# A two-layer encoder on one core: state products from split operands, and a key-norm sum in another PSUM bank

## The chip, the cores and the metric

One NeuronCore of one Trainium2 chip runs the whole program. Its engines have a queue each and meet through semaphores: TensorE (PE in the profile, its weight loads PEld), VectorE (DVE), ScalarE (ACT), GpSimd (POOL), and SyncE (SP), which issues nearly all DMAs. The metric is the device time of one execution in microseconds; less is better.

## The reference, cut to what matters

Two sequences of 512 tokens, each behind 16 learned tokens (528 columns), go through two layers of width 1024.

Layer 1 is a bidirectional gated delta rule with 8 heads. Per head and direction a state `S` (128 x 256) is carried over chunks of tokens, and each chunk uses it twice, with its keys and with its queries:

```
v_new = u_c - w_c @ S
o = qg_c @ S + attn_c @ v_new
S = S * exp(gl_c) + kd_c.T @ v_new
```

Layer 2 is attention with 16 heads; its keys are normalised per head before the scores:

```
k = concatenate([k_nope, k_pe]);  k = k * rsqrt(mean(k * k) + eps) * gain
o = softmax(q @ k.T * scale) @ v
```

The result has to be accurate, so most products are made of split operands: a float32 value is written as a high part `H` (rounded to float32r) and a low part `L` (the rest), and a product is the sum of three float32r passes, H*H, L*H and H*L. A product of plain float32 operands is one instruction in the program and two in the profile.

## The kernel before, in words

Instructions are recorded in Python order and then ordered for every engine by a planner with a timing model of its own; an earlier recorded instruction has priority, those under `high_priority` (helper `pri`) are taken as if recorded so many places earlier, and the planner may take any later recorded one whose inputs and buffers are ready. On the chip each engine then runs its list strictly in that order. `issue_after(x)` makes what is recorded under it stand behind `x` on x's engine. Buffers belong to tags (`BUFS1`, `BUFS2` in SBUF, `PBUFS1`, `PBUFS2` for PSUM banks); a tag with one buffer serves its users in turn.

**Layer 1** (`run`, loop over i from 0 to 15) has 16 units, 8 heads for each of the two sequences. For unit i the scan `gdn_scan` is recorded under high priority, and between its ten steps (5 chunks, 2 directions) pieces of later units are recorded as filling: `gdn_front(i+2)`, which projects, convolves and prepares keys and queries (tile `kq`, conv at L364), `gdn_v(i+1)`, `gdn_z(i+1)`, and under i = 14 and 15 the output projection `out_proj` of the first sequence. A scan starts by splitting two tiles per direction (`kd`, `at`: high part on ACT at L663, low part on POOL through helper `sub`, L87). Each step then goes from engine to engine:

- L682, PE: keys times `S`, plain float32, into bank `ch0` or `ch1`; L684, DVE: `r`
- L693, PE: `r` times the chunk's inverse; L696, ACT, and L697, DVE: its high and low part `vH`, `vL`
- L700, PE: queries times `S`, plain float32, into bank `po`
- L80 to L82, PE (helper `mm3v`): three passes with `vH`, `vL` for the new state and three for the output; L709, DVE: the new `S` (in the first chunk L707, a copy on ACT)
- L719 and L720: the output is taken from `po` and summed.

Projections are streams of float32r passes (helper `mm3`, L74 to L76) into the two banks of tag `pj`; their weights are loaded by SP, rounded by ACT (L213), and their low part is made by POOL (L87).

**Layer 2** (`head`, `pair_scores`, `pair_out`) works by pairs of heads, 16 pairs over both sequences. While the eight tiles of scores of one pair are worked on, the next pair is prepared in steps. `pair_k` projects the keys, ACT and POOL make their squares (L961 to L963), PE sums these over the channels (L966) into the one bank of tag `x`, DVE scales the sums (L967), POOL takes the root (L91), and two DMAs write the result `rk` to DRAM and read it back over all partitions as `rs`. `pair_knorm` multiplies with `rs`: the rope part `kp` on POOL (L1033), then its split `kst` on ACT (L1035); the keys on DVE (L1030), then their split `kH` on ACT. It is recorded in `head` behind two instructions: the last weight split on POOL (`last_wl`) and the last maximum of scores on DVE (`last_mx`). `pair_z` evicts its projection from a `pj` bank by ACT and DVE (L1046, L1047). Bank `x` also serves `pair_out` (the product with the values, L74 to L76 and L1099, released by DVE at L1100) and `pair_q` (L995).

Of the kernel before, what the change touches and what calls it, by code (L numbers as in the profile page):

```python
# [17 lines left out]
T = 528  # L18
# [5 lines left out]
class Trunk:  # L24
    def __init__(self, ctx, tc, ins, outs):
        self.tc, self.nc, self.ins, self.outs = tc, tc.nc, ins, outs
        self.ctx = ctx
        self.cn = ctx.enter_context(tc.tile_pool(name="cn", bufs=1))
        self.dr = ctx.enter_context(tc.tile_pool(name="dr", space=DRAM, bufs=1))
        self.sa = ctx.enter_context(tc.tile_pool(name="sa", bufs=1, reuse_waits="tile"))  # L30
        self.n = 0
        self.inner = None
        self.last_mx = None
        self.next_pool(self.BUFS1, self.PBUFS1)

    def next_pool(self, bufs, pbufs):
        if self.inner is not None:
# [4 lines left out]
        self.ps = self.inner.enter_context(self.tc.tile_pool(name="ps", space=PSUM, bufs=1, reuse_waits="tile"))  # L42

    BUFSA = dict(hnH=1, hnL=1, wraw=3, wh=3, wl=3, acc=4, raw=2)
    BUFS1 = dict(kq=4, kd0=2, kd1=2, kn=3, qe=4, bp=4, ssq=2, vt=2, zs=3, T1=1, X1=1, ms=3,
                 D=2, B=2, Dm=2, Q=1, oa=2, S0=1, S1=1, r=2, ot=1, vH=3, vL=3, osq=2, y=2, ss=4, rs=4, sq=2, 
                 beta=2, gg=2, gh=2, gl=2, ex=2, ne=2, gm=2)
    BUFS2 = dict(sqr=2, kss=2, ce=2, rk=2, sqH=1, sqL=1, kH=3, kL=3, qH=3, qL=3, kst=2, zs=3, qs=4, P=2, SQ0=2, SQ1=2, mx=3, sm=3)
    PBUFS2 = dict(pj=2, S=2, tr=1, x=1)
    PBUFS1 = dict(pj=2, tr=2, lv=1, ch0=1, ch1=1, po=1)  # L50
# [578 lines left out]
    def gdn_scan(self, u, yd, pend):  # L629
        nc = self.nc  # L630
        V, A, PE = nc.vector, nc.scalar, nc.tensor
        h, g, kq, kd, ms, qe, bp, at, XF, vt, zs = (
            u[k] for k in ("h", "g", "kq", "kd", "ms", "qe", "bp", "at", "XF", "vt", "zs"))
        ex = g["ex"]
        yv = yd[2 * h:2 * h + 2].rearrange("k p c -> p k c")
        at_tile = {i: (c0, n) for i, c0, n in self.tiles()}

        def out(i):
            c0, n = at_tile[i]
            sq = self.mO if i == 4 else self.t("osq", [128, 256])  # L640
            m = 80 if i == 4 else 128
            ss = self.t("ss", [128, 1])
            A.activation(sq[:n], oa[:n, i], AF.Square, accum_out=ss[:n])
            V.tensor_scalar(ss[:n], ss[:n], 1.0 / 256, qe[:n, i:i + 1], op0=ALU.mult, op1=ALU.add)
            rs = self.t("rs", [128, 1])
            self.rsqrt(rs[:n], ss[:n])
            A.activation(sq[:n], oa[:n, i], AF.Copy, scale=rs[:n])
            ps = self.p("po", [128, 2, m])
            for hf in range(2):
                PE.transpose(ps[:, hf], sq[:m, 128 * hf:128 * hf + 128], self.ident[:m, :m])  # L650
            y = self.t("y", [128, 2, 128])
            V.tensor_tensor(y[:, :, 0:n], ps[:, :, 0:n], zs[:, :, c0:c0 + n], op=ALU.mult)
            nc.sync.dma_start(yv[:, :, c0:c0 + n], y[:, :, 0:n])

        oa = self.t("oa", [128, 5, 256])
        G = nc.gpsimd
        at2, kd2 = [], []
        for d in range(2):
            n = 3 + d
            for nm, src, m, res in (("kd", kd[d], n, kd2), ("at", at[:, 4 * d:4 * d + 4], 4, at2)):  # L660
                hi = self.t("%sH%d" % (nm, d), [128, m, 128], F32R)
                lo = self.t("%sL%d" % (nm, d), [128, m, 128], F32R)
                A.copy(hi[:, 0:m], src[:, 0:m])  # L663
                self.sub(G, lo[:, 0:m], src[:, 0:m], hi[:, 0:m])
                res.append((hi, lo))
        mW, mR, mV = self.mW, self.mR, self.mV
        A.copy(mW[0:16], ms)
        A.copy(mW[32:48], ms)
        self.sub(V, mW[64:80], ms, mW[0:16])
        seen = set()  # L670
        S = [self.t("S%d" % d, [128, 256]) for d in range(2)]
        order = ([4, 0, 1, 2, 3], [3, 2, 1, 0, 4])
        for k in range(5):
            for d in range(2):
                i = order[d][k]
                n = NM if i == 4 else 128
                c0 = 0 if i == 4 else NM + 128 * i
                sl = slice(c0, c0 + n)
                pc = self.p("ch%d" % d, [128, 2, 256])
                r = vt[:n, i]  # L680
                if k > 0:
                    PE.matmul(pc[:n, 0], kq[:, 0, sl], S[d], start=True, stop=True)  # L682
                    r = self.t("r", [128, 256])[:n]
                    V.scalar_tensor_tensor(r, pc[:n, 0], g["ne"][:n, d, i, h:h + 1], vt[:n, i], op0=ALU.mult, op1=ALU.add)  # L684
                b = bp[:n, i, d:d + 1]
                if i == 4:
                    self.stack(mR, r)
                    PE.matmul(pc[:n, 1], mW[:, 32 + 16 * d:48 + 16 * d], mR, start=True, stop=True)
                    A.activation(mV[0:16], pc[:n, 1], AF.Copy, scale=b)
                    A.activation(mV[64:80], pc[:n, 1], AF.Copy, scale=b)  # L690
                    V.scalar_tensor_tensor(mV[32:48], pc[:n, 1], b, mV[0:16].bitcast(F32), op0=ALU.mult, op1=ALU.subtract)
                else:
                    PE.matmul(pc[:n, 1], XF[:, 4 * d + i], r, start=True, stop=True)  # L693
                    vH = self.t("vH", [128, 256], F32R)
                    vL = self.t("vL", [128, 256], F32R)
                    A.activation(vH, pc[:, 1], AF.Copy, scale=b)  # L696
                    V.scalar_tensor_tensor(vL, pc[:, 1], b, vH.bitcast(F32), op0=ALU.mult, op1=ALU.subtract)  # L697
                po = self.p("po", [128, 2, 256])
                if k > 0:
                    PE.matmul(po[:n, 0], kq[:, 1, sl], S[d], start=True, stop=True)  # L700
                if k < 4:
                    if i == 4:
                        PE.matmul(pc[:, 0], mW[:, 64:192], mV, start=True, stop=True)
                    else:
                        self.mm3v(pc[:, 0], [x[:, i] for x in kd2[d]], (vH, vL))
                    if k == 0:
                        A.copy(S[d], pc[:, 0])  # L707
                    else:
                        V.scalar_tensor_tensor(S[d], S[d], ex[:, 2, d, i, h:h + 1], pc[:, 0], op0=ALU.mult, op1=ALU.add)  # L709
                if i == 4:  # L710
                    PE.matmul(po[:n, 1], mW[:, 16 * d:16 * d + 16], mV, start=True, stop=True)
                else:
                    self.mm3v(po[:, 1], [x[:, i] for x in at2[d]], (vH, vL))
                e = ex[:n, 0, d, i, h:h + 1]
                if k == 0:
                    A.copy(oa[:n, i], po[:n, 1])
                else:
                    t = self.t("ot", [128, 256])[:n] if i in seen else oa[:n, i]
                    A.copy(t, po[:n, 1])  # L719
                    V.scalar_tensor_tensor(t, po[:n, 0], e, t, op0=ALU.mult, op1=ALU.add)  # L720
                    if i in seen:
                        G.tensor_tensor(oa[:n, i], oa[:n, i], t, op=ALU.add)  # L722
                seen.add(i)
                yield
            ready = pend if k == 0 else {3: [1], 4: [0, 2]}.get(k, [])
            for f in ready:
                f() if k == 0 else out(f)
        pend[:] = [lambda i=i: out(i) for i in (3, 4)]
# [217 lines left out]
    def pair_k(self, u):  # L946
# [8 lines left out]
        for j, h in enumerate(hs):  # L955
# [5 lines left out]
            A.activation(kk[o], kr[nn, j], AF.Square)  # L961
            A.activation(sq[o], kr[o, j], AF.Square)
            G.tensor_tensor(kk[o], kk[o], sq[o], op=ALU.add)  # L963
        ps = self.p("x", [88, 6, 2])
        for i in range(6):
            PE.matmul(ps[:, i], kk[:, 88 * i:88 * i + 88], self.two, start=True, stop=True)  # L966
        V.scalar_tensor_tensor(rk, ps.rearrange("p i j -> p j i"), 1.0 / 192, c["kss"].unsqueeze(1).to_broadcast([88, 2, 6]), op0=ALU.mult, op1=ALU.add)  # L967
# [81 lines left out]
    def pair_scores(self, u, j, qt):  # L1049
# [15 lines left out]
        V.tensor_scalar(mx, mx, qs[j][:, qt:qt + 1], None, op0=ALU.mult)  # L1065
        P = self.t("P", [128, 2, 264])
        sm = self.t("sm", [128, 1])
        A.activation(P, Sv, AF.Exp, bias=mx, scale=qs[j][:, qt:qt + 1], accum_out=sm)  # L1068
        V.reciprocal(sm, sm)
        P = P.rearrange("p a b -> p (a b)")  # L1070
        V.tensor_scalar(P, P, sm, None, op0=ALU.mult)
# [32 lines left out]
    def run(self, rc, rs):  # L1104
# [27 lines left out]
        v, z, inv = (lambda i: self.gdn_v(U[i])), (lambda i: self.gdn_z(U[i])), (lambda i: self.gdn_inverse(U[i]))  # L1132
        for f in (front(0), front(1), self.pri(inv(0), 1000), v(0), z(0)):
            drain(f)
        tL1 = ("kq", "kq", "kq", "B", "B", "zs", "vt", "oa")
        tA, tC = ("hnH", "hnL"), ("h2H", "h2L")
        rsd = [self.d("rsd", [1, T]) for _ in range(2)]
        pss = [[], []]
# [9 lines left out]
        for i in range(16):  # L1148
# [11 lines left out]
            for n, _ in enumerate(self.pri(self.gdn_scan(U[i], y1[units[i][0]], pend), 100)):  # L1160
                if n > 0:
                    next(iv, None)
                for _ in range(((1, 1, 1, 1, 1, 1, 1, 1, 1, 1) if i == 15 else (3, 3, 1, 2, 1, 2, 2, 3, 2, 2))[n]):
                    next(fill, None)
            drain(iv)
            if i != 15:
# [14 lines left out]
        def head(u):  # L1181
# [10 lines left out]
                yield  # L1192
            self.pair_q(u, 1)
            with ExitStack() as behind:
                for x in [self.last_wl] + ([self.last_mx] if self.last_mx is not None else []):
                    behind.enter_context(self.tc.issue_after(x.ins))
                self.pair_knorm(u, 0)
                self.pair_knorm(u, 1)
# [105 lines left out]
```

## Time and profile before

| | before |
|---|---|
| median of 3 runs | 2698.04 us (2696.45 to 2699.07) |
| profiled execution, time | 2700.19 us |
| profiled execution, span of its trace | 2698.5 us |
| TensorE clock granted, mean share | 0.957 |
| busy: PE, PEld, DVE, ACT, POOL | 93%, 83%, 65%, 54%, 47% |

Busy PE time counts matmuls that overlap in the array, so 93% is not 93% of its rate. Layer 1 fills the span to about 1350 us, layer 2 the rest. The rate of a stream is read from the starts of its instructions in the timeline, not from their durations. Times in queries are counted from the start of the span.

### The profile page before, as it was taken

Reading aid. Unit: us, or ns where it says so; the run is one execution under the profiler, and the core shown is the slowest. Engines: PE = TensorE matmul, PEld = TensorE weight load, DVE = VectorE, ACT = ScalarE, POOL = GpSimd, SP = SyncE. Lnnn points to the kernel's source line nnn. Section 1 sums busy time; section 2 is a strip of 40 time slices with the busy share of each in tenths; the row PEclk is TensorE's granted clock in tenths of the full one; section 3 lists DMA queues with packets and bytes.
Section 4 is the critical chain, followed back from the end, with each engine's and each line's share of the span. In section 5 each row is a group of like instructions: output and inputs, shape, how many; then the busy total and the mean of one; then the engine's idle time right before and its main releaser. Section 6 shows DMA issues by size and latency. Waiting matters only on the chain. (4 is left out here: it accounts for less than half of the span.)

```text
span 2698.5 us, 51896 instructions
## 1 busy us (share of the span) xinstructions
PE 2500.3 (93%) x19083; PEld 2237.2 (83%) x19083; DVE 1755.9 (65%) x3915; ACT 1452.6 (54%) x3522; POOL 1270.0 (47%) x1255
## 2 busy tenths in 40 slices
PE   8899999999999999899999999998998989999999
PEld 7888888878888888788989888887887878887787
DVE  6888887777897777886554356555665656566421
ACT  5445555556555555645545466555556555655432
POOL 5544554435445444533445555444436454544243
PEclk9999999989999999989999899999999999999999
DMA  3222222221222243225475423232322322225475
GB/s 101 67 51 59 56 62 57 70 61 48 62 63 59 53 125 83 78 70 152 121 229 160 125 73 80 67 66 73 91 79 76 79 67 71 66 66 152 136 231 148
DMA packets 448511, 245.14 MB, mean 91 GB/s; under 512 B 131132, under 2 KB 408878, under 8 KB 448256
## 3 DMA queue, kind: packets, MB, share of 16 engines
q1 hardware_dynamic: 448256, 241.82, 33.6%
q8 instruction: 150, 2.46, 0.4%
q14 instruction: 105, 0.86, 0.1%
HBM read 190.72 MB, written 42.08 MB: 86 GB/s over the span
## 5 line engine op out<-in xcount | busy, mean ns | idle before, releaser
L87 POOL TENSOR_TENSOR wl<-wraw,wh 128x512 fp32r<-128x512 f32 (+2 forms) x512 | 661.5, 1294 | 805.4 <-ACT wh L213 744.4
L74 PE MATMUL pj<-hnH,wh 128*128 128x264 f32 (+4 forms) x2080 | 634.1, 306 | 20.0 <-DVE zs L624 10.6
L76 PE MATMUL pj<-hnH,wl 128*128 128x264 f32 (+3 forms) x2080 | 633.6, 306 | 0.5 <-POOL wl L87 0.5
L75 PE MATMUL pj<-hnL,wh 128*128 128x264 f32 (+3 forms) x2080 | 628.9, 303 | 4.5 <-DVE hnL L774 4.5
L213 ACT CAST wh<-wraw 128x512 fp32r<-128x512 f32 (+2 forms) x512 | 306.9, 602 | 312.7 <-PE pj L75 203.2
L74 PEld LDWEIGHTS pj<-hnH,wh 128*128 128x128 f32 (+1 forms) x2080 | 402.5, 194 | 37.6 <-DVE zs L624 12.5
L75 PEld LDWEIGHTS pj<-hnL,wh 128*128 128x128 f32 (+1 forms) x2080 | 402.7, 194 | 18.6 <-DVE hnL L774 5.1
L76 PEld LDWEIGHTS pj<-hnH,wl 128*128 128x128 f32 (+1 forms) x2080 | 401.9, 193 | 15.5 <-issue 3.7
L74 PE MATMUL pj<-h2H,wh 128*128 128x512 f32 (+1 forms) x544 | 207.0, 383 | 5.0 <-ACT h2H L769 3.0
L76 PE MATMUL pj<-h2H,wl 128*128 128x512 f32 (+1 forms) x544 | 207.3, 382 | 0.0
L75 PE MATMUL pj<-h2L,wh 128*128 128x512 f32 (+1 forms) x544 | 206.2, 380 | 0.7 <-DVE h2L L87 0.7
L1064 DVE TENSOR_REDUCE mx<-S 128x1 f32<-128x528 f32 x128 | 89.7, 702 | 77.1 <-PE S L1061 76.7
L74 PEld LDWEIGHTS pj<-h2H,wh 128*128 128x128 f32 x544 | 103.1, 191 | 24.7 <-ACT h2H L769 3.5
L364 DVE SCALAR_TENSOR_TENSOR acc<-raw,vec,acc 128x528 f32<-128x528 f32 x128 | 117.5, 921 | 4.4 <-ACT acc L362 3.3
L75 PEld LDWEIGHTS pj<-h2L,wh 128*128 128x128 f32 x544 | 103.2, 190 | 18.9 <-DVE h2L L87 2.1
L76 PEld LDWEIGHTS pj<-h2H,wl 128*128 128x128 f32 x544 | 103.4, 190 | 17.9 <-POOL wl L87 0.2
L1068 ACT ACTIVATE P<-S,mx,qs 128x528 f32<-128x528 f32 x128 | 101.2, 790 | 31.0 <-DVE mx L1065 29.9
L364 DVE SCALAR_TENSOR_TENSOR kq<-raw,vec,kq 128x528 f32<-128x528 f32 x128 | 110.6, 864 | 9.4 <-ACT kq L362 8.4
L783 DVE TENSOR_TENSOR raw<-raw,pj 128x512 f32<-128x512 f32 (+1 forms) x54 | 31.2, 580 | 125.1 <-PE pj L76 117.8
L722 POOL TENSOR_TENSOR oa<-oa,ot 128x256 f32<-128x256 f32 (+1 forms) x80 | 68.2, 853 | 81.1 <-DVE ot L720 80.9
L87 DVE TENSOR_TENSOR hnH<-tr,hnH 128x512 fp32r<-128x512 f32 x128 | 87.8, 686 | 27.6 <-ACT hnH L1091 26.0
L494 DVE TENSOR_TENSOR Yt<-Bl,Y 66x15 f32<-66x15 f32 (+7 forms) x240 | 85.5, 356 | 23.4 <-POOL Bl L486 18.9
(483 smaller groups left out, 6848.2 us busy)
## 6 DMA issues: line engine op xcount, KB each, us to landing
wraw<-in_gdn_w_in_dram SPq DMA_DIRECT2D x192, 256.0 KB
wraw<-in_mla_w_in_dram SPq DMA_DIRECT2D x88, 256.0 KB
wraw<-in_gdn_w_out_dram SPq DMA_DIRECT2D x64, 256.0 KB
wraw<-in_mla_w_out_dram SPq DMA_DIRECT2D x64, 256.0 KB
acc<-y SPq DMA_DIRECT2D x32, 264.0 KB
rs<-rkd SPq DMA_DIRECT2D x16, 528.0 KB
y<-y SPq DMA_DIRECT2D x64, 128.0 KB
wraw<-in_mla_w_ukv_dram SPq DMA_DIRECT2D x64, 128.0 KB
```

What stands on the lines that cost most here:

```text
L74: mm(out, ah, bh, start=first, stop=False)
L75: mm(out, ah, bl, start=False, stop=False)
L76: mm(out, al, bh, start=False, stop=last)
L87: return eng.tensor_tensor(out, a, hi, op=ALU.subtract)
L213: nc.scalar.copy(wh, raw)
L364: nc.vector.scalar_tensor_tensor(acc, raw[:, j:j + T], self.convw(j, u), acc, op0=ALU.mult, op1=ALU.add)
L494: V.tensor_tensor(tv, Bl[:, r + 1:16, r:r + 1].to_broadcast([66, m, c]), Y[:, r:r + 1, 0:c].to_broadcast([66, m, c]), op=ALU.mult)
L722: G.tensor_tensor(oa[:n, i], oa[:n, i], t, op=ALU.add)
L783: nc.vector.tensor_tensor(r[:, c0:c0 + chunk], r[:, c0:c0 + chunk], ps, op=ALU.add)
L1064: self.last_mx = V.tensor_reduce(mx, Sv, axis=AX.XY, op=ALU.max, negate=True)
L1068: A.activation(P, Sv, AF.Exp, bias=mx, scale=qs[j][:, qt:qt + 1], accum_out=sm)
```

## The change

- Keys and queries are split once per unit (`kqH`, `kqL`, one buffer each), the high part on ACT, the low part on POOL. After each update of `S` two more instructions make `SH` (ACT) and `SL` (DVE). L682 and L700 become three float32r passes each.
- Room for the new tiles: `kq` has 2 buffers instead of 4, `vL` 2 instead of 3, `Dm`, `osq` and `gm` 1 instead of 2. The output projection of the first sequence, which borrowed three `kq` tiles for its second half, borrows two and `kqH`; in the last scan's two last steps no filling is recorded any more.
- The sum over the squared keys goes to a `pj` bank instead of `x`.
- `pair_knorm` also stands behind `last_P`, the exponential (ACT) of the latest tile of scores recorded before it.

```diff
-        self.last_mx = None
+        self.last_mx = self.last_P = None
...
-    BUFS1 = dict(kq=4, ... vL=3, osq=2, ... Dm=2, ... gm=2)
+    BUFS1 = dict(kq=2, ... vL=2, osq=1, ... Dm=1, ... gm=1)
...
+        kqH, kqL = (self.t(x, [128, 2, T], F32R) for x in ("kqH", "kqL"))
+        for j in range(2):
+            A.copy(kqH[:, j], kq[:, j])
+            self.sub(G, kqL[:, j], kq[:, j], kqH[:, j])
...
+        SH = [self.t("SH%d" % d, [128, 256], F32R) for d in range(2)]
+        SL = [self.t("SL%d" % d, [128, 256], F32R) for d in range(2)]
...
-                    PE.matmul(pc[:n, 0], kq[:, 0, sl], S[d], start=True, stop=True)
+                    self.mm3v(pc[:n, 0], (kqH[:, 0, sl], kqL[:, 0, sl]), (SH[d], SL[d]))
...
-                    PE.matmul(po[:n, 0], kq[:, 1, sl], S[d], start=True, stop=True)
+                    self.mm3v(po[:n, 0], (kqH[:, 1, sl], kqL[:, 1, sl]), (SH[d], SL[d]))
...
+                    s_in = pc[:, 0] if k == 0 else S[d]
+                    A.copy(SH[d], s_in)
+                    self.sub(V, SL[d], s_in, SH[d])
...
-        ps = self.p("x", [88, 6, 2])
+        ps = self.p("pj", [88, 6, 2])
...
-        A.activation(P, Sv, AF.Exp, bias=mx, scale=qs[j][:, qt:qt + 1], accum_out=sm)
+        self.last_P = A.activation(P, Sv, AF.Exp, bias=mx, scale=qs[j][:, qt:qt + 1], accum_out=sm)
...
-        tL1 = ("kq", "kq", "kq", "B", "B", "zs", "vt", "oa")
+        tL1 = ("kq", "kq", "B", "B", "zs", "vt", "oa", "kqH")
...
-  for _ in range(((1, 1, 1, 1, 1, 1, 1, 1, 1, 1) if i == 15 else (3, 3, 1, 2, 1, 2, 2, 3, 2, 2))[n]):
+  for _ in range(((1, 1, 1, 1, 1, 1, 1, 1, 0, 0) if i == 15 else (3, 3, 1, 2, 1, 2, 2, 3, 2, 2))[n]):
...
-                for x in [self.last_wl] + ([self.last_mx] if self.last_mx is not None else []):
+                for x in [self.last_wl] + ([self.last_mx, self.last_P] if self.last_mx is not None else []):
```

## Rows read from the trace of the kernel before

**Rows 1.** Page, part 4: the chain that ended last, by engine.
```profile
PE 9%; DMA 1%; ACT 1%; DVE 1%; issue 0%; SPq 0%; POOL 0%; ACTq 0%; POOLq 0%
```

**Rows 2.** Windows: busy us (instructions) of PE, PEld, DVE, ACT, POOL; clock; DMA.
```profile
207.00:1228.00 1021.00, 965.03 (x8777) 864.12 (x8774) 814.98 (x2014) 571.12 (x1567) 490.40 (x584) 0.95 0.27 68
1303.00:1351.00 48.00, 47.66 (x346) 43.97 (x344) 25.09 (x55) 25.04 (x57) 18.08 (x19) 1.00 0.44 127
1560.00:2440.00 880.00, 793.15 (x5031) 707.37 (x5030) 530.57 (x1070) 511.14 (x1152) 415.47 (x311) 0.95 0.29 74
1740.00:1765.00 25.00, 24.48 (x171) 22.06 (x170) 15.20 (x34) 13.49 (x33) 10.06 (x8) 1.00 0.31 52
1765.00:1785.00 20.00, 13.99 (x85) 12.86 (x84) 10.79 (x24) 10.90 (x26) 8.17 (x6) 0.83 0.25 79
```

**Rows 3.** Waits of PE in layer 2, 1560 to 2440: us in total, times, longest.
```profile
PE pj L74 <- DVE zs L1047: 34.9, 8, 5.7
PE pj L74 <- DVE hnL L87: 16.5, 3, 7.4
```

**Rows 4.** Waits of the other engines in the same stretch.
```profile
POOL acc L1033 <- DMA rs<-rkd: 85.8, 13, 9.7
ACT kst L1035 <- POOL acc L1033: 85.3, 13, 7.5
```

**Rows 5.** Timelines of POOL, PE and ACT, one pair: start, us, instruction, [idle before].
```profile
1727.43 1.33 POOL L963 TENSOR_TENSOR sqH<-sqH,raw 64x528 f32<-64x528 f32 x1 [1.41 <-ACT raw L962]
...
1748.35 0.29 PE L1099 MATMUL x<-pst,vst 80*128 80x256 f32 x1
...
1750.84 1.03 PE L966 MATMUL x<-two,sqH 128*88 128x2 f32 x12
...
1753.73 2.28 POOL L91 TENSOR_TENSOR rk<-rk,mhalf 88x12 f32<-88x12 f32 x1
...
1767.90 2.55 POOL L1033 TENSOR_TENSOR acc<-kpr,rs 128x528 f32<-128x528 f32 x2 [6.50 <-DMA rs<-rkd]
...
1769.23 0.63 ACT L1035 CAST kst<-acc 128x528 fp32r<-128x528 f32 x1 [6.80 <-POOL acc L1033]
...
1771.65 0.59 PE L74 MATMUL pj<-ckvH,wh 128*128 128x264 f32 x1 [5.04 <-DVE zs L1047]
```

**Rows 6.** Timeline of PE in layer 1, around one product with the state.
```profile
707.41 0.28 PE L75 MATMUL pj<-hnL,wh 128*128 128x256 f32 x1
707.53 0.59 PE L682 MATMUL ch<-S,kq 128*128 128x256 f32 x2
707.78 0.47 PE L76 MATMUL pj<-hnH,wl 128*128 128x256 f32 x1
708.09 0.28 PE L74 MATMUL pj<-hnH,wh 128*128 128x256 f32 x1
```

**Rows 7.** The two lines by source: count, ns min/median/max, first and last start.
```profile
L682 PE MATMUL ch<-S,kq x256: 377/379/795, 133.9 to 1342.3; 128*128 128x256 f32 x112, 128*16 128x256 f32 x16
L700 PE MATMUL po<-S,kq x256: 377/379/797, 149.1 to 1351.2; 128*128 128x256 f32 x112, 128*16 128x256 f32 x16
```

**Rows 8.** Groups by line and shape: busy us, mean ns | idle before.
```profile
L697 DVE SCALAR_TENSOR_TENSOR vL<-ch,bp,vH 128x256 fp32r<-128x256 f32 x128 | 60.8, 476 | 19.1 <-ACT vH L696 18.5
L213 ACT CAST wh<-wraw 128x256 fp32r<-128x256 f32 x32 | 12.8, 403 | 20.2 <-issue 7.7 <-POOL wl L87 7.5 <-PE pj L75 4.3
L378 ACT CAST kH<-kr 128x528 fp32r<-128x528 f32 x32 | 20.2, 632 | 25.8 <-DVE kr L1030 25.7
L87 POOL TENSOR_TENSOR atL<-D,atH 128x512 fp32r<-128x512 f32 x32 | 44.7, 1397 | 5.8 <-ACT atH L663 4.3 <-PE ch L693 1.5
```

**Rows 9.** Waits of PE in layer 1, 207 to 1228.
```profile
PE ch L682 <- DVE S L709: 6.0, 11, 1.4
```

**Rows 10.** Timeline of DVE in layer 1: two like instructions of two SBUF inputs.
```profile
883.25 1.23 DVE L494 TENSOR_TENSOR Yt<-Bl,Y 66x60 f32<-66x60 f32 x1
...
885.04 0.21 DVE L494 TENSOR_TENSOR Yt<-Bl,Y 66x55 f32<-66x55 f32 x1
```

More of the change, by code (lines that the diff above doesn't have):

```diff
@@ L44 @@
     BUFSA = dict(hnH=1, hnL=1, wraw=3, wh=3, wl=3, acc=4, raw=2)
-    BUFS1 = dict(kq=4, kd0=2, kd1=2, kn=3, qe=4, bp=4, ssq=2, vt=2, zs=3, T1=1, X1=1, ms=3,
-                 D=2, B=2, Dm=2, Q=1, oa=2, S0=1, S1=1, r=2, ot=1, vH=3, vL=3, osq=2, y=2, ss=4, rs=4, sq=2,
-                 beta=2, gg=2, gh=2, gl=2, ex=2, ne=2, gm=2)
+    BUFS1 = dict(kq=2, kd0=2, kd1=2, kn=3, qe=4, bp=4, ssq=2, vt=2, zs=3, T1=1, X1=1, ms=3,
+                 D=2, B=2, Dm=1, Q=1, oa=2, S0=1, S1=1, r=2, ot=1, vH=3, vL=2, osq=1, y=2, ss=4, rs=4, sq=2,
+                 beta=2, gg=2, gh=2, gl=2, ex=2, ne=2, gm=1)
     BUFS2 = dict(sqr=2, kss=2, ce=2, rk=2, sqH=1, sqL=1, kH=3, kL=3, qH=3, qL=3, kst=2, zs=3, qs=4, P=2, SQ0=2, SQ1=2, mx=3, sm=3)
```

## The prediction

> **What bounds the kernel now.** I read four views in this order. The chain that ended last comes first, and is of little use: its shares add up to 12% of the span [rows 1], so the way back was lost. The windows by stage come next. In layer 1 PE is busy for 965 of 1021 us and DVE for 815, which is 80% [rows 2] (its first row); PE's 56 idle us there are spread over many short waits. In layer 2 PE is busy for 793 of 880 us, 87 idle [rows 2] (third row), and here two waits stand out: PE waits 34.9 us in 8 times for DVE's eviction of pair_z's projection, and 16.5 us in 3 for that of pair_v's [rows 3]. The waits of the other engines say why: POOL waits 13 times for the DMA that brings `rs`, and ACT 13 times for POOL's product with it, 85 us each [rows 4].
>
> The timeline of one pair shows the whole chain [rows 5]. POOL ends the squares at 1728.8 (1727.43 + 1.33). The sums over them, which need only these and a bank, run at 1750.84, 22 us later, 2.5 us after the last pass of an older product with the values (L1099, 1748.35) that used the one bank of tag `x`. The root ends at 1756.0; two DMAs later, 11.9 us on, POOL can make `kp` at 1767.90, having waited 6.50. ACT stood 6.80 at `kst`, and behind `kst` in its list stands the eviction that frees a `pj` bank; so PE stood 5.04. After that the clock falls: in the 25 us before, PE had 1.00 of its clock, in the 20 us that hold the wait 0.83 [rows 2] (last two rows). That is 6.8 us at 1.2 instead of 2.4 GHz (34% of 20), and a loss of 0.17 x 20 = 3.4 us, after an engine that had stood still for 5.
>
> **The change part by part.** The profiled execution took 2700.2 us; the sum is made against it.
>
> *Products with S.* From the start of a single pass (707.41) to the start of the product is 0.12; from there to 708.09 lie the product and one single pass, 0.56 [rows 6]. So a plain float32 product costs PE 0.56 - 0.12 = 0.44, and three passes cost 3 x 0.118 = 0.354 (weights are loaded anew in both). Each of the two lines has 256 instructions, two to a product [rows 7], so there are 256 products: 256 x 0.086 = **-22 us** of PE's time, in a stage where PE is the busiest engine. I take it whole. At the least it is 0, where PE would wait instead.
>
> *Splits that are added.* DVE gets 128 `SL` at 0.48 (the like `vL`, 476 ns), ACT 128 `SH` at 0.40 and 32 `kqH` at 0.63, POOL 32 `kqL` at 1.44 (1397 ns x 528/512) [rows 8]: 61, 71 and 46 us over 16 units. ACT and POOL have room: both were busy about half of layer 1. DVE has little. In the window 13 units of the 16 lie, so DVE goes from 815 to 865 of 1021; its free share shrinks from 20.2% to 15.3%. My estimate is that PE's idle time in layer 1 grows as that share shrinks, since most links of a scan pass through DVE: 56 x (20.2/15.3 - 1) = 18, for 16 units **+22 us**. The ends: 0, if the planner puts the new links beside filling, since now L682 waits for `S` only 6.0 us in 11 times [rows 9]; and +121, if every one of the 64 chunk steps (16 units, 4 chunks, the two directions side by side) is longer by `SH`, `SL` and a blocked DVE instruction: 0.40 + 0.48 + 1.0 = 1.9, the 1.0 from two like instructions of which one took 1.23 and the other 0.21 [rows 10]. I stay near the lower end because a scan's links are now covered by projections.
>
> The Trainium skill, page "SBUF — State Buffer", section "Who interferes with whom", says that a DVE instruction with two SBUF inputs and a GpSimd instruction that reads SBUF lock each other out for a whole instruction; the trace agrees with those two rows. By that rule 7 of 8 `SL` would wait, at POOL's share of 0.48, for half of 1.4 us, 0.34 each; DVE would be at 88%, the term +46 and the time 24 us above my forecast, an estimate.
>
> *Buffers.* With two `kq`, `gdn_front(i+2)` may write only after POOL's two `kqL` of scan i: covered by the key projection and other filling; without cover 2 x 1.44 x 16 = 46 us. One `gm`, one `osq` and two `vL` make POOL, ACT and DVE wait for PE now and then. I take 0 for all of them, with 30 as the upper end, since none is on the way to a PE instruction that lacks other work beside it.
>
> *End of layer 1.* In the last scan PE is full, 47.66 of 48 us at clock 1.00 [rows 2] (second row). The scan's own part is 8 steps x (three products at 0.44, six passes) = 8 x 2.03 = 16, the other 31 are output projection, pulled forward by the planner. Now the eighth pair of its second half lies in `kqH`, read until the scan's last L700 at 1351 [rows 7]; its load (one DMA on SP, one ACT, one DVE instruction) comes after, and the products stop after seven pairs in both `pj` banks: 2 x 21 x 0.118 = 5 us. So 26 us of filling move behind the scan, while the scan, alone on PE, needs some 20 to 24 us (nine links of about 0.45, and their hops, in four chunks) instead of 48. These nearly cancel: **+3 us**, ends -4 and +10.
>
> *The sums in a `pj` bank, and last_P.* Two `pj` banks are free soon after ACT has taken the last key projection. So the sums run some 2 us after the squares, not 22, and `rs` is back at about 1748 in that pair, 13 us before POOL came to `kp` (1767.90 - 6.50 = 1761.4) [rows 5]. And `kst` goes behind a later exponential, so even a late `rs` no longer keeps ACT from evicting. Each edit alone takes the wait from ACT, the first also from POOL. What goes: the two waits of [rows 3] without the longest of them, 34.9 + 16.5 - 7.4 = **-44 us**; I leave that one in, since it may be the start of a sequence, where no older pair holds `x`. Behind these ten waits the clock falls: 10 x 3.4 = **-34 us**; the whole stretch loses (1 - 0.95) x 880 = 44 that way [rows 2], so this fits in. What is late next: `kst` and two `kH` (0.63 each [rows 8]) now crowd on ACT right before the next pair's scores, and while a `pj` bank holds the sums the other projections have one bank, so that PE sees an eviction of about 1.1 us. 0.6 + 1.1 for 14 pairs is **+24 us**; the ends are 0 and 14 waits as long as now, 70.
>
> *Sum.* -22 + 22 + 3 - 44 - 34 + 24 = -51: 2649 for an execution like the profiled one. That one lay 2.2 us above the median of the runs (2698.0), so I predict **2647 us**. Nearly all of it comes from layer 2.
>
> **Rivals.** (1) *The wait in layer 2 only moves.* The planner orders by its own times, and it placed `kp` 6.5 us too early for the DMAs that it has to wait for [rows 4, 5]; with earlier sums it may place `kp` earlier too, or keep the bank waiting. Then POOL stands, the weight splits behind `kp` are late, and PE waits for those. Against it: `last_wl` keeps `kp` from moving far ahead. A third of the 78 us is gained, the 24 stay: -22 + 22 + 3 - 26 + 24 = +1, 2699 us (2680 to 2705). This includes that the sums don't run earlier at all.
>
> (2) *The scan waits for SL; slower than before.* Place: the third pass of L682 and L700, in each of 64 chunk steps. Price: up to 1.9 us each, +121 instead of +22, which gives 2700.2 - 2.2 - 22 + 121 + 3 - 78 + 24 = 2746. It decides from 73 us on, that is 1.1 us of uncovered wait per step, where it has used up all other gains. For it: DVE is already at 80%, and like instructions are held up by a microsecond. Against it: the present link from `S` costs almost nothing.
>
> (3) *Everything is covered.* No new wait on DVE, nothing late next in layer 2, the end of layer 1 even: -22 - 78 = -100, 2598 us.
>
> **How the numbers follow.** Forecast 0.50, its own range 2615 to 2680; rival 1 0.17, rival 2 0.16, rival 3 0.17. About 0.2%, 5.4 us, is what a measurement here can tell from no change: faster is below 2692.6, slower above 2703.4. Faster: 0.50 + 0.17 + 0.05 of rival 1 + 0.02 of rival 2 = 0.74; same 0.08 + 0.01 = 0.09; slower 0.04 + 0.13 = 0.17. The range 2595 to 2712 leaves out most of rival 2 (0.12) and the lower tail of rival 3 (0.07).
>
> **What would show it.** Products: starts of L682's three passes 0.12 apart. Layer 2: L966 within a few us of the squares; the waits ACT kst <- POOL acc and PE pj <- DVE zs near 0, and a granted clock near 0.98 in 1560 to 2440. Layer 1: PE's idle time per unit within a few us of now, DVE near 85%, waits for `SH` and `SL` no longer than those for `S`. It would be wrong if the last scan ended later than now (rival 2), or if POOL's wait for `rs` stayed and PE waited for weight splits (rival 1).

## The result and the profile after

The changed kernel takes 2837.69 us (median of 4 runs, 2836.75 to 2848.11) where the kernel before takes 2698.56: 1.0537 times as long (95% interval 1.0509 to 1.0566). I had predicted 2647, faster. The profiled execution has a span of 2846.1 us at a mean clock of 0.919.

The windows of the kernel after, over the first stretch of [rows 2] and over 880 us from the start of layer 2, which begins 127.5 us later than before (busy us of PE, PEld, DVE, ACT, POOL; clock; DMA share; GB/s):

```profile
207.00:1228.00 1021.00, 918.31 (x8189) 840.41 (x8189) 814.53 (x1916) 570.44 (x1572) 476.58 (x566) 0.87 0.24 60
...
1690.00:2570.00 880.00, 776.67 (x4912) 692.70 (x4913) 554.84 (x1052) 496.70 (x1131) 420.89 (x305) 0.94 0.27 72
```

In layer 1 PE does less in the same time (8189 instructions, before 8777) and its clock is 0.87, before 0.95. DVE is as busy as before, not busier.

By stages, bounded by the starts of the first scan's first `mW` copy, of the last scan's, and of the first and the last exponential of scores; "slow clock" is the sum of the trace's stretches granted 1.2 GHz instead of 2.4, up to the first exponential:

| us | to the first scan | 15 scans | last scan to first exponential | layer 2 | slow clock |
|---|---|---|---|---|---|
| before | 107.5 | 1192.6 | 262.5 | 978.6 | 126 |
| after | 123.3 | 1284.7 | 282.2 | 987.4 | 345 |

So layer 1 and its end lost 127.5 us, and layer 2, which was to gain 54, lost 9. Another 11 stand behind the last exponential (168.5 us, before 157.2): 715 PE instructions start there, before 667, so a part of this is work left over from layer 2. Counted to the end of the program, layer 2 lost 20.

**Layer 2.** The waits of the kernel after, 1690 to 2841 (us in total, times, longest):

```profile
POOL acc L944 <- DMA acc<-acc: 89.7, 14, 8.2
...
DVE acc L946 <- POOL acc L945: 83.4, 14, 7.7
...
PE S L1092 <- DVE P L1080: 58.8, 19, 5.9
...
POOL acc L1042 <- DMA rs<-rkd: 5.3, 1, 5.3
```

Two of these in the kernel before, 1563 to 2541:

```profile
POOL acc L935 <- DMA acc<-acc: 17.6, 13, 3.2
...
PE S L1083 <- DVE P L1071: 4.1, 5, 1.5
```

POOL's wait for `rs` is gone, as predicted (5.3 us, before 85.8 [rows 4]), and ACT's for `kst` with it. In its place POOL waits as long for another DMA: `swap` in `pair_qrope`, which exchanges halves of the rotary part of the queries. DVE waits for POOL there, and PE for the softmax weights `P`, which stand behind that sum in DVE's list. One pair's timeline shows why:

```profile
1870.44 1.10 PE L975 MATMUL pj<-two,sqH 128*88 128x2 f32 x12 [0.25 <-POOL sqH L972]
...
1874.30 0.32 SPq L980 DMA_DIRECT2D rkd<-rk  x1
...
1876.82 0.69 ACT L939 ACTIVATE acc<-pj,vec 128x512 f32<-128x512 f32 x1
...
1880.69 0.34 SPq L982 DMA_DIRECT2D rs<-rkd  x1
...
1882.22 2.47 SPq L839 DMA_DIRECT2D acc<-acc  x4
...
1887.06 1.29 POOL L944 TENSOR_TENSOR acc<-acc,rc 128x512 f32<-128x512 f32 x1 [5.90 <-DMA acc<-acc]
...
1889.63 1.73 DVE L946 TENSOR_TENSOR acc<-acc 128x512 f32<-128x512 f32 x1 [5.44 <-POOL acc L945]
...
1891.96 0.85 DVE L1080 TENSOR_SCALAR P<-P,sm 128x528 f32<-128x528 f32 x1
...
1892.96 0.37 PE L1092 MATMUL S<-ident,P 128*16 128x128 f32 x1 [3.63 <-DVE P L1080]
```

The sums come early. But SP issues its list in order, and `rs<-rkd` waits for the store of 1874.30: it goes out 6.39 us later. The four DMAs of the swap stand behind it (and behind one store of a result, at 1881.08). Their input was ready at 1877.51 (1876.82 + 0.69); they start at 1882.22, 4.7 us late. SP's own waits show this load for all pairs, first after (1690 to 2841), then before (1563 to 2698):

```profile
SPq L982 <- DMA rkd<-rk: 85.6, 15, 6.4
...
SPq L973 <- DMA rkd<-rk: 88.4, 15, 7.1
```

SP stood as long before, but then the swap had gone out ahead of the store: in all 16 pairs it starts at most 0.39 us after its input. In the kernel after, 12 of 16 start 3.2 to 5.2 us late.

**Layer 1.** When `kq` may be written. ACT's timeline in the kernel before, up to the second scan (unit 1): the first writes of unit 3's keys and queries (L362), whose front is recorded as filling of this scan, and the scan's first copy (L667).

```profile
175.00 0.74 ACT L362 ACTIVATE kq<-raw,vec 128x528 f32<-128x528 f32 x1
...
190.32 0.73 ACT L362 ACTIVATE kq<-raw,vec 128x528 f32<-128x528 f32 x1
...
212.92 0.33 ACT L667 CAST mW<-ms 16x192 fp32r<-16x192 f32 x1
```

The same in the kernel after (the scan's copy is L671 there), and POOL's timeline with `kqL`, which frees the buffer:

```profile
219.22 0.35 ACT L671 CAST mW<-ms 16x192 fp32r<-16x192 f32 x1 [0.28 <-PE po L720]
...
223.89 1.34 ACT L362 ACTIVATE kq<-raw,vec 128x528 f32<-128x528 f32 x2
```

```profile
218.49 2.68 POOL L87 TENSOR_TENSOR kqL<-kq,kqH 128x528 fp32r<-128x528 f32 x2 [1.19 <-ACT kqH L668]
```

Before, the writes come 38 and 23 us ahead of the scan; after, 4.7 us behind its start, once POOL has ended the second `kqL` at 221.2. It is so in every later unit but one (unit 8, the first of the second sequence): from unit 3 on, the first write comes 26 to 66 us ahead of the scan before, and 1 to 13 us behind its start after. So projections run dry: they go from a `pj` bank to a tile `raw`, of which there are two, and a `raw` is free again only when the keys or queries have been made from it. ACT's next such copy waits for that:

```profile
235.81 0.38 ACT L358 COPY raw<-pj 128x264 f32<-128x264 f32 x1 [0.26 <-DVE kq L367]
```

Windows of the kernel after, and as a fourth line one of the kernel before around the same scan's start; the first fence is all work, the second (PE, PEld, DVE, ACT) that on tiles `pj` alone:

```profile
172.00:208.00 36.00, 32.62 (x326) 28.24 (x325) 27.25 (x86) 15.79 (x40) 11.53 (x12) 0.95 0.17 35
208.00:240.00 32.00, 25.74 (x274) 20.79 (x275) 24.21 (x60) 20.41 (x59) 10.30 (x16) 0.52 0.08 22
240.00:290.00 50.00, 47.44 (x369) 45.20 (x367) 41.85 (x94) 24.26 (x66) 26.81 (x29) 1.00 0.20 49
...
201.00:233.00 32.00, 29.46 (x291) 25.91 (x292) 28.78 (x62) 20.97 (x61) 19.47 (x26) 0.87 0.19 51
```

```profile
172.00:208.00 36.00, 12.67 (x73) 10.55 (x73) 0.00 (x0) 0.75 (x2) 0.95 0.17 35
208.00:240.00 32.00, 0.79 (x2) 0.55 (x2) 0.00 (x0) 0.78 (x2) 0.52 0.08 22
240.00:290.00 50.00, 36.09 (x251) 32.64 (x251) 1.67 (x4) 3.42 (x9) 1.00 0.20 49
...
201.00:233.00 32.00, 16.20 (x100) 14.88 (x101) 0.42 (x1) 1.50 (x4) 0.87 0.19 51
```

From 208 to 240 PE has two instructions of projection, otherwise links of the scan and the inverse, and a clock of 0.52; before, 100 and 0.87. Nearly the same stands at 980 to 1010 (20 of projection, clock 0.54). Between the first scan's start and the last's, PE is without a projection for more than 12 us at a time on 10 occasions, 242 us in all; before on 2, 51 us.

### The profile page after: what moved, and what is told of

It reads as the page before. It is cut to its first block, busy times and chain, and to the rows that moved or that the text cites. A ratio compares the mean times of both kernels' runs of the same rounds, so it can differ in the third digit from the quotient of the medians.

```text
span 2846.1 us, 52877 instructions
## 1 busy us (share of the span) xinstructions
PE 2556.9 (90%) x19339; PEld 2311.7 (81%) x19339; DVE 1883.9 (66%) x4043; ACT 1508.4 (53%) x3682; POOL 1328.6 (47%) x1287
## 5 line engine op out<-in xcount | busy, mean ns | idle before, releaser
L74 PEld LDWEIGHTS pj<-hnH,wh 128*128 128x128 f32 (+1 forms) x2080 | 408.8, 197 | 35.2 <-DVE P L792 7.7
L75 PEld LDWEIGHTS pj<-hnL,wh 128*128 128x128 f32 (+1 forms) x2080 | 408.6, 196 | 10.4 <-DVE hnL L87 0.7
L1100 ACT CAST hnH<-tr 128x512 fp32r<-128x512 f32 x128 | 75.0, 586 | 99.3 <-PE tr L1094 97.5
L494 DVE TENSOR_TENSOR Yt<-Bl,Y 66x15 f32<-66x15 f32 (+7 forms) x240 | 110.4, 460 | 15.6 <-POOL Bl L486 10.5
L91 POOL TENSOR_TENSOR rs<-ss,mhalf 128x1 f32<-128x1 f32 (+1 forms) x80 | 54.4, 685 | 135.4 <-DVE ss L644 125.5
```

Source lines behind the costliest of these rows:

```text
L74: mm(out, ah, bh, start=first, stop=False)
L75: mm(out, ah, bl, start=False, stop=False)
L91: self.nc.gpsimd.tensor_tensor(out, a, self.mhalf[:n, 0:a.shape[1]], op=ALU.pow)
L494: V.tensor_tensor(tv, Bl[:, r + 1:16, r:r + 1].to_broadcast([66, m, c]), Y[:, r:r + 1, 0:c].to_broadcast([66, m, c]), op=ALU.mult)
L1100: A.copy(PTH[:, :, hc], pt)
```

## The experiments

Ratios are to runs of the kernel before on the same chip, with 95% intervals; chips differ by up to 0.7%, so ratios are compared and not times. 1% is 27 us.

### The two halves of the change

`l1_only` is the change without its last two diff parts (`pj` for the sums, `last_P`); `l2_only` is these two alone.

> The layer-1 part of the change alone (products from split operands, the smaller buffers, the end of layer 1); layer 2 as before. In the two traces the first attention weights come 127.5 us later (1562.4 to 1689.9) and the layer-2 loop is 8.8 us longer, so if the two parts add, this kernel takes 2698 + 128 to 139 = 2826 to 2837 us. If the layer-2 edits made room for, or took time from, the work around the end of layer 1, it would lie outside 2815 to 2845.

Measured 1.0437 (1.0417 to 1.0457).

> The layer-2 part alone (key norm sums in a projection bank, key norms issued behind the last exponentials too); layer 1 as before. If the two parts add and the waits were only exchanged (POOL's and ScalarE's waits of 92 us gone, TensorE's wait for the normalised weights up from 4.9 to 58.8 us), 2700 to 2710 us. If the edit gains by itself as my prediction had it and the longer first layer spoilt it, 2640 to 2670 us.

Measured 1.0046 (1.0023 to 1.0069). The parts come to 4.4 + 0.5 of 5.4%; the other 0.5%, 14 us, shows only with both together and is not explained. Layer 2 loses by itself; a longer first layer isn't the cause.

### Layer 2: what stands in the new place

```diff
# l2_rope_late = l2_only, and in head(), before pair_v:
+            with tc.issue_after(self.last_P.ins):
+                self.pair_qrope_tail(u)   # L935 and below, cut out of pair_qrope
```

> The layer-2 edits alone plus one move: the last part of the queries' rotary step (two products on GpSimd, the sum on VectorE, the splits) is issued two steps later and behind the last exponential. Theory D: VectorE stands at the rotary sum (84.9 us in 14 waits) for the swapped copy that comes back by DMA 10.2 us after it was written, with the softmax's reciprocal and normalisation queued behind it, and TensorE waits for them (59.0 us); before, the wait for the key norms' DMA in the same slot hid this one. Then the move takes away both: 50 us of TensorE's stalls and part of the low clock after them, 2635 to 2675 us, and the first layer as before. If TensorE's filling, not VectorE's order, is what runs out, the wait goes elsewhere again and it takes 2700 to 2720 us.

Measured 1.0070 (1.0044 to 1.0096): the move didn't help, and "theory D" as put there fell. VectorE stood as long at the sum, now elsewhere in its list. SP's queue in this run shows the cause that I had not looked at:

```profile
1875.66 0.32 SPq L977 DMA_DIRECT2D rkd<-rk  x1
1876.93 0.55 SPq L830 DMA_DIRECT2D acc<-acc  x1
1882.10 0.33 SPq L979 DMA_DIRECT2D rs<-rkd  x1
1882.47 1.81 SPq L830 DMA_DIRECT2D acc<-acc  x3
```

The load of `rs` cuts the swap in two: one of its DMAs goes out before, three after a stop of 5 us. So only SP's order was changed next:

```diff
# l2_swap_first = l2_only, and
-        nc.sync.dma_start(rs, rkd...)          # in pair_k
+        with self.tc.issue_after(self.last_swap.ins):
+            nc.sync.dma_start(rs, u["rkd"]...)  # in pair_qrope, after swap
```

> The layer-2 edits alone, and the load that spreads the key norms is issued behind the four copies of the queries' rotary swap in SP's queue; the order of every other engine stays as in the kernel with the layer-2 edits alone. There, in each pair, SP stood 6.8 us at this load (issued at 1873.10 for a store of 1866.34), and the swap, whose input was ready at 1869.55, went out from 1873.97 on, 4.4 us late. Theory D' (SP's queue): the swap goes out 4.4 us earlier, the rotary sum on VectorE waits 1 to 2 us per pair and no longer 6, TensorE's wait for the normalised weights falls from 59 to under 20 us, and the time is 2650 to 2680 us where before takes 2698 (ratio 0.982 to 0.993), the first layer as before. If the swap's own way takes the time, or filling runs out on TensorE: ratio 1.000 to 1.007, as without the move.

Measured 0.9875 (0.9856 to 0.9894): 2651.76 us where before took 2685.66 on that chip. This kernel beats both. Its waits in layer 2, and SP and its followers in one pair:

```profile
POOL acc L938 <- DMA acc<-acc: 29.0, 15, 2.5
...
DVE acc L940 <- POOL acc L939: 22.2, 14, 2.1
...
PE S L1085 <- DVE P L1073: 19.3, 13, 1.7
```

```profile
1887.59 0.32 SPq L974 DMA_DIRECT2D rkd<-rk  x1
...
1890.10 0.69 ACT L930 ACTIVATE acc<-pj,vec 128x512 f32<-128x512 f32 x1
...
1890.82 2.45 SPq L830 DMA_DIRECT2D acc<-acc  x4
...
1894.46 0.33 SPq L937 DMA_DIRECT2D rs<-rkd  x1
...
1896.08 1.29 POOL L938 TENSOR_TENSOR acc<-acc,rc 128x512 f32<-128x512 f32 x1 [1.64 <-DMA acc<-acc]
```

The swap goes out 0.03 us after its input (1890.10 + 0.69), here and in the 15 other pairs, and the later load is waited for once (DVE, 3.9 us). Layer 2 takes 925.0 us, 53.6 less than before; 164.0 follow, where 157.2 did, so 47 are left at the program's end. The runs say less, 34 us: the profiled execution was the fastest of the six.

The same move on the changed kernel:

> The changed kernel with the key norms' load issued behind the rotary swap in SP's queue, nothing else. With the layer-2 edits alone this move took the ratio to before from 1.0046 to 0.9875, that is 46 us. If SP's queue is the whole of layer 2's story, the changed kernel falls from 1.0537 to 1.034 to 1.040 (2790 to 2808 us where before takes 2698), and what is left is layer 1 alone. If layer 2 of the changed kernel is held by something else too: 1.045 or more.

Measured 1.0303 (1.0279 to 1.0326): 2.3% come back, more than the 1.4 to 2.0% that I expected from SP's queue and than the 1.7% without layer 1's edits. What remains comes from layer 1.

### Layer 1: the buffers

`bufs_only`: the kernel before with the `BUFS1` and end-of-layer lines of the diff, plain products, no splits (in the borrowed list an otherwise unused `kqH`).

> The smaller buffers of layer 1 (kq 4 to 2, gm, osq, Dm 2 to 1, vL 3 to 2) and the changed end of layer 1 alone, with the plain fp32 products and no splits, layer 2 as before. Theory A (kq with two buffers lets no later front be pulled forward, so the projections run out at the unit's edge): nearly all of the loss is here, 2780 to 2840 us, and the TensorE stretches without a projection at half clock stand in it. But without the splits a kq is held until the scan ends, so A can even be worse here than in the changed kernel. Theory B (the splits and their waits in the scan cost the time): 2695 to 2715 us.

Measured 1.0750 (1.0725 to 1.0775), 2900 us where before takes 2698: above A's range and worse than the whole change, as the expectation says it can be. Without splits `kq` is held to the scan's end, and in the trace the writes come where the next scan starts.

```diff
# kq3_no_low = after, and
-    kq=2
+    kq=3
-        kqH, kqL = ...
+        kqH = kqL = self.t("kqH", [128, 2, T], F32R)   # and no kqL subtraction
```

> The changed kernel with kq in three buffers instead of two. For room the low part of the keys and queries is left out (the pass with it reads the high part again, so TensorE does the same passes; GpSimd makes 32 subtractions of 128x528 less). Theory A (kq's buffers): most of the 128 us of layer 1 comes back, 2710 to 2750 us. Theory B (splits of the state, DVE and ScalarE in the scan's chain): 2810 to 2840 us. If the subtraction on GpSimd is what delays the scan (a third way): also near 2710 to 2750, and a run with two buffers and no low part must tell it from A.

Measured 1.0242 (1.0226 to 1.0258): at before's 2698 this is 2763 us, 13 above A's range and 47 below B's. One more `kq` gives back 2.95 of the 5.37%, 80 us; with it `kq` comes free when the scan before starts, as early as with four before. The sum of the slow clock falls from 345 to 195 us. That GpSimd also makes 32 subtractions less was not tried apart, by two `kq` without them; in the trace of the kernel after PE waits nowhere by name for `kqL` (100 to 1440).

`kq3_plain`: the kernel before with `kq=3`, one number changed.

> The kernel before with kq in three buffers instead of four, nothing else changed. Theory A': what counts is when the buffer for the keys and queries of unit i+2 comes free. Before: when scan i-2 ends, which is when scan i-1 starts. In the changed kernel: once scan i has split its operands. Here: when scan i-1 ends, which is when scan i starts, so nearly as in the changed kernel; with two buffers and no splits it was the end of scan i, one scan later, and that cost 168 us between the first scan's start and the last's. By A' the units here are as slow as in the changed kernel (+92 us from the first scan's start to the last's), 2760 to 2800 us in all, with the layer's clock down as there. Theory B (the splits, or the small buffers, make the changed kernel's units slow): under 2715 us.

Measured 1.0266 (1.0232 to 1.0301), within A' as a whole, but not as it was put: the 15 scans take 1231.6 us (+39, not +92), and the end of the layer 293.3 (+31), probably since three borrowed `kq` are now all there are. That the buffer's release sets when the next front is written is shown by the trace, where the write now comes with the scan, 4 us before its first copy, and no longer 38 us ahead of it (ACT L362 and L667):

```profile
205.63 1.36 ACT L362 ACTIVATE kq<-raw,vec 128x528 f32<-128x528 f32 x2
...
209.57 0.35 ACT L667 CAST mW<-ms 16x192 fp32r<-16x192 f32 x1
```

The small cuts were then made on the kernel before, which keeps four `kq`: all four (`small_bufs`: vL=2, osq=1, gm=1, Dm=1), and with one given back.

> The kernel before with the four small buffer cuts alone (vL 3 to 2; gm, osq and Dm 2 to 1); kq keeps four. Theory A': 2698 to 2710 us. Theory C (the small buffers are what is left over of the loss when kq gets its third buffer back, 20.6 us in the units): 2715 to 2740 us. My prediction's bound for them was 0 to 30 us.

Measured 1.0139 (1.0107 to 1.0171); the 15 scans take 1218.5 us, +26.

> The kernel before with the small cuts of vL (3 to 2), osq (2 to 1) and Dm (2 to 1) alone; gm keeps two buffers. With gm cut too the ratio was 1.0139, and GpSimd waited 41.2 us, up to 13.8 at a time, for TensorE to be done with the one gm, in order ahead of its other work; before, that wait was not among its ten largest. If gm's cut is the price: 0.997 to 1.005. If ScalarE's wait for the one osq (25.1 us before, 42.3 with the cuts) or vL is: 1.008 to 1.014.

Measured 1.0145 (1.0119 to 1.0171): not `gm`, though GpSimd waited 41.2 us for it in `small_bufs`.

> The kernel before with vL cut from 3 to 2 and gm and Dm from 2 to 1; osq keeps two buffers. All four cuts: 1.0139. With one osq, ScalarE waits for TensorE's transposes of the last one (13.4 us in 14 waits; 2.1 before) with all that stands behind it on ScalarE. If osq is the price: 0.998 to 1.006. If not: 1.009 to 1.017.

Measured 1.0072 (1.0046 to 1.0098): `osq` makes about half of it. The wait is small, but it is ScalarE's, in front of all that it does for the scan; first the run with one `osq` (`small_gm2`), then that with two, 100 to 1400:

```profile
ACT osq L643 <- PE po L650: 13.4, 14, 2.5
```

```profile
ACT osq L643 <- PE po L650: 5.2, 6, 1.5
```

> The kernel before with osq, gm and Dm cut from 2 to 1; vL keeps three buffers. With two, VectorE waits for TensorE's products (vL from po: 8.0 us in 5 waits; none before), and it is in the scan's chain. If vL is the price: 0.998 to 1.006; if not: 1.009 to 1.017. If neither this nor the run with osq given back comes down, it is Dm, or each of them a part by the planner's other order.

Measured 1.0135 (1.0107 to 1.0163): not `vL`. The other half isn't settled: `Dm` was not given back by itself.

### Layer 1: its end

`kq3_old_end` is `kq3_no_low` with the borrowed list (`"kq", "kq", "kq"`) and the filling counts of before.

> The kernel with three kq buffers and no low part of keys and queries, with the end of layer 1 as it was (the output projection's operands in three kq buffers, and a filling step behind each of the last two scan steps). The time from the last scan's start to the first attention weights was 262.5 us before, 282.2 in the changed kernel and 283.7 in the kernel with three kq buffers. If the edit at the end costs that, it falls back to about 263 and the total by some 20 us, to 2745 to 2755 us. If the end is late because the work before it changed, the total stays at 2765 to 2775 us.

Measured 1.0256 (1.0220 to 1.0292): no difference that these runs can tell. In the profiled executions the stretch from the last scan to the first exponential went from 283.7 to 270.6 us, 13 of the 21 that were lost. So the trace is for the edit costing some 13 us, and the times don't confirm it.

### Layer 1: the products and their splits

`kq3_no_state_low` is `kq3_no_low` without `SL` (`SL = SH`).

> The kernel with three kq buffers and no low part of keys and queries, and without the low part of the state too: its third pass reads the high part, so TensorE does the same passes, VectorE makes 128 subtractions of 128x256 less (0.43 us each by the trace, 55 us of its time). The waits that TensorE spent for the state's parts in that kernel were 4.8 us (high) and 4.4 us (low) beside 14.2 us for vL. If the state's split on VectorE costs what its place in the chain suggests, the time falls by 5 to 25 us against the kernel with three kq buffers (ratio to before 1.0242): 1.015 to 1.022. If it is hidden: 1.022 to 1.027.

Measured 1.0198 (1.0177 to 1.0219): 0.44%, 12 us, for `SL`.

`products_free` is `kq3_no_state_low` with vL=3, osq=2, Dm=2, the old end, and the load behind the swap.

> The products from split operands with nothing of their price in buffers: three kq (freed when the scan starts, as early as with four before), vL, osq and Dm as before, the end of layer 1 as before, layer 2 with the key norms' load behind the swap. For the room the low parts of keys, queries and state are left out; the passes with them read the high parts, so TensorE does the same passes. To be held against the layer-2 edits with that load alone, ratio 0.9875. If the products give their 22 us (256 times 0.44 less 0.354) and the splits that are left (64 on ScalarE for the state, 32 for keys and queries) are hidden: 0.977 to 0.982. If those splits take the gain back: 0.984 to 0.992. If the products' other order costs more than that: above 0.993.

Measured 0.9974 (0.9949 to 0.9998), against 0.9875 without the products: 1.0% or 27 us more, the third case. `gm` has one buffer here and two there (`small_gm2` found no price for that). The two kernels from the start to the first exponential, first without the products, then with them:

```profile
0.00:1552.40 1552.40, 1456.94 (x12864) 1324.40 (x12864) 1138.27 (x2683) 844.54 (x2179) 757.19 (x872) 0.97 0.33 88
```

```profile
0.00:1593.80 1593.80, 1465.02 (x13120) 1349.62 (x13120) 1150.09 (x2683) 898.38 (x2339) 757.28 (x872) 0.95 0.32 86
```

With the products PE has 256 instructions more, is busy for 8 us more and idle for 33 more, and the slow clock sums to 164 us where it is 106 without them. Half of these 58 us, 29, is what the clock cost if PE was busy in all of them; then the work itself got 21 us less (8 - 29), an estimate. The two runs were on chips whose runs of the kernel before are 0.6% apart, so some 10 of the 41 us between these lines are the chips'. One link could be tried by itself:

```diff
# products_direct = products_free, and for k > 0
-                    A.copy(SH[d], S[d])                      # after S's update
+                    V.scalar_tensor_tensor(SH[d], S[d], ex..., pc[:, 0], ...)  # before it
```

> The kernel with the products free of their price in buffers, and the state's high part made by VectorE straight from the product (the same instruction as the state's own update, with the rounded output, ahead of it) in place of ScalarE's copy of the finished state; low parts left out as there. The chain from the product to the next three passes then has one instruction, as with plain fp32; VectorE has 96 instructions of 0.48 us more. If ScalarE's link (0.40 us and its hops, in 48 steps that have a state to copy, some 30 to 40 us at most) is what costs: ratio 0.982 to 0.990, with TensorE's waits for it (6.1 us in 5, by name) gone. If VectorE's share or the planner's other order costs: 0.994 to 1.003.

Measured 1.0028 (1.0011 to 1.0046), no better. So taking ScalarE's link out of the chain does not give the time back; but the edit puts 96 instructions on VectorE, which may cost what the link did. Whether the price is VectorE's share or the other order that the planner makes stays open.

## Why the prediction was wrong

**The step that failed is "Buffers"**, priced at 0 with 46 for `kq` and up to 30 for the small ones as its ends. Measured: the cut of `kq` from four to three, which frees it about as late as the changed kernel does, costs 2.7%, 72 us, by itself (`kq3_plain`), and a third `kq` in the changed kernel (with 32 subtractions less) gives back 80; the four small cuts cost 1.4%, 38 us. The mechanism was written down ("`gdn_front(i+2)` may write only after POOL's two `kqL` of scan i"), and then priced by the two POOL instructions in the way. That was the wrong quantity. The buffer comes free a whole scan later than before; the convolutions of the next front, which began 26 to 66 us ahead of the scan, can't be pulled forward, and it is the projections into and behind them that fill PE while the scan waits on its own chain. "Covered by the key projection and other filling" took for cover what the edit takes away.

*Products, -22, and splits, +22.* The three passes of this product start 0.20 and 0.12 us apart in PE's timeline of the kernel after, a little wider than the 0.118 that I took (medians over 232 such triples: 0.126 and 0.120):

```profile
767.18 0.36 PE L80 MATMUL ch<-SH,kqH 128*128 128x256 f32 x1
...
767.38 0.28 PE L81 MATMUL ch<-SH,kqL 128*128 128x256 f32 x1
767.50 0.28 PE L82 MATMUL ch<-SL,kqH 128*128 128x256 f32 x1
```

The splits have about the sizes that I gave them (groups by line and shape, 100 to 1440: busy us, mean ns | idle before):

```profile
L87 DVE TENSOR_TENSOR SL<-S,SH 128x256 fp32r<-128x256 f32 x96 | 53.5, 557 | 16.0 <-PE po L82 10.4 <-ACT SH L717 5.0
...
L87 DVE TENSOR_TENSOR SL<-ch,SH 128x256 fp32r<-128x256 f32 x32 | 13.2, 415 | 2.0 <-ACT SH L717 1.9
```

That is 67 us of DVE, estimated 61, and PE's waits by name for `SH` and `SL` are 2.5 and 1.9 us in all (100 to 1440), less than for `S` before [rows 9]. The 96 that read `S` and `SH` took 0.14 us longer than the 32 that read a bank; my estimate of a lock-out had 0.34. DVE is at 80% in layer 1 and not at 85%, since the layer got longer. So rival 2's place was wrong. But together the two terms came to +27 us without most of the splits (`products_free`), where they were to be 0 with all of them: the gain on PE is not there as time. By the estimate above its work got less by about what I forecast, and a lower clock and more idle time took more than that; why PE idles more is open.

*End of layer 1, +3 (-4 to +10).* The stretch is 20 us longer; about 13 of it by the edit, if the profiled executions are right.

*Layer 2, -44 - 34 + 24 = -54.* The sums run as soon as the squares are there (PE stood 0.25 us for them) and the waits named went (PE pj <- DVE zs: 0.7 us, once), but the clock in layer 2 is 0.94 (1690 to 2570) where I wanted 0.98. With SP's order mended (`l2_swap_first`) the gain is 53.6 us in the profiled layer 2, 47 to the program's end and 34 by the runs; the changed kernel got none of it. Rival 1, "the wait in layer 2 only moves", is what happened (layer 2 +9 us, +20 to the program's end; its price was -26 + 24 = -2), though not in the form that I gave it: POOL stood for the swap and not for `rs`. What I left out is SP. A sum that runs 20 us earlier also issues its store and its load 20 us earlier, and there the list of SP held the swap; a load that waits for a store holds up all behind it.

The account closes: `l1_only` times `l2_swap_first`, 1.0437 x 0.9875 = 1.0306, is what `after_swap_first` measured (1.0303), and the 2.3% from there to 1.0537 are SP's order. Of these, 1.7% appear with layer 2's edits alone; why the same order costs 0.6% more behind the longer layer 1 was not looked into.

## What to carry to other kernels

When a buffer count is cut, ask when the buffer comes free and what may then no longer run ahead; price that work as filling lost, not the instruction that frees it. When a step moves earlier, follow its DMAs into the issuing queue as well: a load that waits for its own store blocks every DMA behind it in that engine's list (6 us a pair here), and an order that puts such a load last can be worth more than the edit.

## What the runs showed of the hardware that I had not expected

PE's clock fell to 0.52 for 32 us although PE was busy for 25.74 of them (208 to 240 above), after 36 us at 0.95; what had gone is the projections, and with them (47.44 of 50 us busy) it was back at 1.00. And the same sum of 128x512 on VectorE took 0.69 us (median of 15) before and 1.73 where the moved order put it beside GpSimd's subtraction of weights. In the kernel before, the nine sums with no GpSimd instruction beside them took 0.67 to 0.69 us and the other seven 1.01 to 2.66; after, all 16 have one beside them and took 1.73 to 1.78. The Trainium skill, page "SBUF — State Buffer", section "Who interferes with whom", says that a DVE instruction with two SBUF inputs contends with a GpSimd instruction that reads SBUF; these numbers agree.
